# Reordering the stores and loads of one DMA queue in an RMSNorm kernel that repeats its rows

## The chip, the core and the metric

The kernel runs on one core of a Trainium2 chip. The metric is the device time of one execution in microseconds, over several timed runs. A profiled execution of each kernel gives the trace. Its span is some 1.7 to 1.8 us shorter than the timed figure, so spans are compared with spans and times with times.

## The reference

```python
def reference(x, gamma):                      # x: 8 x 512 x 2048, float32
    x_rep = np.repeat(x, 2, axis=1)           # each row twice
    rms = np.sqrt((x_rep ** 2).mean(axis=-1, keepdims=True) + 1e-6)
    return (x_rep / rms * gamma[None, None, :]).astype(np.float32)
```

The input is 33.6 MB, the output, with each row twice, 67.1 MB.

## The kernel before

Eight tiles of 512 rows. A tile occupies a buffer of 128 partitions x 8 rows; the load (4.19 MB) fills the upper four rows, the compute writes each row's result twice over the buffer, the store (8.39 MB) sends all eight rows out. There are three buffers, so load 3 must wait until store 0 has landed, load 4 for store 1, and so on. All large transfers are issued by SP, one after the other in program order: when SP waits for one issue, all issues behind it wait as well.

```python
rows = ctx.enter_context(tc.tile_pool(name="rows", bufs=3))
# ...
def load(i, eng, parts=1):
    y = rows.tile([P, K * R, D], f32, name="y")
    step = K // parts
    for k in range(0, K, step):
        at = K * (R - 1) + k
        eng.dma_start(out=y[:, at : at + step, :], in_=x_t[i, :, k : k + step, :])
    ys.append(y)

def store(i, k0, k1):
    nc.sync.dma_start(out=out_t[i, :, R * k0 * D : R * k1 * D], in_=ys[i][:, R * k0 : R * k1, :] ...)
# ...
def compute(i):
    for k in range(K):
        scale(i, k, square(i, k))             # squares on ACT, scaling on DVE
    repeat(i, 0, K // 2, nc.scalar.copy)      # half of the second copies on ACT
    repeat(i, K // 2, K, nc.vector.tensor_copy)
# ...
load(0, nc.sync, parts=2)
# ... gamma, eps ...
load(1, nc.sync)
load(2, nc.sync)
loads_after = {2: (3, 4, 5), 4: (6, 7)}
for i in range(ntiles):
    compute(i)
    store(i, 0, K)
    for j in loads_after.get(i, ()):
        load(j, nc.sync)
```

## Time and profile before

| What | Before |
|---|---|
| time, median of the first 3 runs | 239.39 us |
| span of the profiled run | 237.9 us |
| share of the span in which the SP queue's packets filled the 16 DMA engines | 98.5% |
| busy share of the vector and the scalar engine | 41%, 42% |

The prediction below shows the main lines. Two more views: the first is the busy tenths of the two compute engines in 40 slices of the span: 9 is busy, 0 is idle.

```profile
DVE  0049999960000000059999960000199990000000
ACT  2697999900000000099999920000599960000000
```

The compute comes in three blocks: tiles 0 to 2, tiles 3 to 5, tiles 6 and 7. Between them both engines stand still for some 30 to 50 us, waiting for a load. The second is the timeline of ACT at the start of the second block; in brackets is the idle time before it and what ended it.

```profile
101.18 1.88 ACT L64 ACTIVATE sq<-y 128x2048 f32<-128x2048 f32 x1 [53.03 <-DMA y<-in_x_dram]
```

ACT stood still for 53.03 us until load 3 landed.

### The profile page before, as it was taken

Reading aid. Unit: us, or ns where it says so; the run is one execution under the profiler, and the core shown is the slowest. Engines: PE = TensorE matmul, PEld = TensorE weight load, DVE = VectorE, ACT = ScalarE, POOL = GpSimd, SP = SyncE. Lnnn points to the kernel's source line nnn. Section 1 sums busy time; section 2 is a strip of 40 time slices with the busy share of each in tenths; the row PEclk is TensorE's granted clock in tenths of the full one; section 3 lists DMA queues with packets and bytes.
Section 4 is the critical chain, followed back from the end, with each engine's and each line's share of the span. In section 5 each row is a group of like instructions: output and inputs, shape, how many; then the busy total and the mean of one; then the engine's idle time right before and its main releaser. Section 6 shows DMA issues by size and latency. Waiting matters only on the chain.

```text
span 237.9 us, 287 instructions
## 1 busy us (share of the span) xinstructions
DVE 96.5 (41%) x73; ACT 101.0 (42%) x106; POOL 2.5 (1%) x5
## 2 busy tenths in 40 slices
DVE  0049999960000000059999960000199990000000
ACT  2697999900000000099999920000599960000000
POOL 0030000000000000000000000000000000000000
DMA  7999998989899998999998999989998989999994
GB/s 265 436 446 441 441 441 353 530 353 496 386 452 430 397 485 353 441 441 441 441 518 364 464 419 430 452 369 430 435 518 364 518 364 485 397 452 430 408 474 176
DMA packets 2464, 100.69 MB, mean 423 GB/s; under 512 B 279, under 2 KB 285, under 8 KB 286
## 3 DMA queue, kind: packets, MB, share of 16 engines
q1 hardware_dynamic: 2448, 100.66, 98.5%
q14 instruction: 2, 0.02, 0.0%
q10 hardware_dynamic: 14, 0.01, 0.0%
HBM read 33.56 MB, written 67.11 MB: 423 GB/s over the span
## 4 chain that ended last, share of the span: by engine, by line
DMA 58%; ACT 12%; DVE 9%; issue 1%; POOLq 1%; ACTq 1%; SPq 0%
DMA y<-in_x_dram 33%; DMA out_dram<-y 21%; ACT sq L64 8%; DVE y L74 7%; DMA gamma_b<-in_gamma_dram 4%; ACT y L81 3%; DVE y L81 2%; ACT rms L68 1%; POOLq L136 1%; ACTq L95 1%; DVE rstd L73 0%; POOLq L96 0%; SPq L56 0%
## 5 line engine op out<-in xcount | busy, mean ns | idle before, releaser
L64 ACT ACTIVATE sq<-y 128x2048 f32<-128x2048 f32 x32 | 59.7, 1865 | 87.8 <-DMA y<-in_x_dram 87.8
L74 DVE SCALAR_TENSOR_TENSOR y<-y,rstd,gamma_b 128x2048 f32<-128x2048 f32 x32 | 75.3, 2352 | 4.1 <-POOL gamma_b L96 3.0
L73 DVE RECIPROCAL rstd<-rms 128x1 f32<-128x1 f32 x32 | 5.0, 158 | 94.6 <-ACT rms L68 94.3
L81 ACT COPY y<-y 128x4096 f32<-128x4096 f32 x8 | 28.7, 3590 | 1.4 <-DVE y L74 1.4
L81 DVE COPY y<-y 128x4096 f32<-128x4096 f32 x8 | 18.3, 2294 | 0.3
L68 ACT ACTIVATE rms<-ss,eps_t 128x1 f32<-128x1 f32 x32 | 9.4, 295 | 1.0
L64 ACT ACTIVATION_READ_ACCUMULATOR sq<-y 128x1 f32 x32 | 6.0, 187 | 0.0
L64 ACT ACT_TABLE_LOAD x1 | 1.3, 1283 | 3.0 <-issue 3.0
L96 POOL PARTITION_BROADCAST gamma_b<-gamma_b x1 | 2.3, 2294 | 12.2 <-DMA y<-in_x_dram 12.2
L68 ACT ACT_TABLE_LOAD x1 | 1.3, 1283 | 0.0
L98 DVE MEMSET eps_t<- 128x1 f32 x1 | 0.1, 59 | 0.8 <-PEq L125 0.8
L125 POOL MEMSET const-uint8-127<- 128x1 uint8 x1 | 0.1, 102 | 0.0
L125 POOL MEMSET const-bfloat16-1.0<- 128x1 bf16 x1 | 0.1, 101 | 0.0
L125 POOL MEMSET const-float32-0.0<- 128x1 f32 x1 | 0.1, 98 | 0.2 <-issue 0.2
L125 POOL MEMSET const-float32-1.0<- 128x1 f32 x1 | 0.1, 98 | 0.0
## 6 DMA issues: line engine op xcount, KB each, us to landing
y<-in_x_dram SPq DMA_DIRECT2D x7, 4096.0 KB, 14.6
y<-in_x_dram SPq DMA_DIRECT2D x2, 2048.0 KB, 7.4
out_dram<-y SPq DMA_DIRECT2D x8, 24.4
gamma_b<-in_gamma_dram ACTq DMA_DIRECT2D x6, 1.0 KB
gamma_b<-in_gamma_dram ACTq DMA_DIRECT2D x1, 2.0 KB
```

The lines of the kernel that those rows point to most:

```text
L64: nc.scalar.activation(out=sq[:], in_=ys[i][:, K * (R - 1) + k, :], func=Act.Square, accum_out=ss[:])
L68: nc.scalar.activation(out=rms[:], in_=ss[:], func=Act.Sqrt, scale=inv_d, bias=eps_t[:])
L73: nc.vector.reciprocal(out=rstd[:], in_=rms[:])
L74: nc.vector.scalar_tensor_tensor(out=ys[i][:, R * k, :], in0=ys[i][:, K * (R - 1) + k, :], scalar=rstd[:], in1=gamma_b[:], op0=Alu.mult, o ...
L81: copy(out=y_r[:, k0:k1, 1, :], in_=y_r[:, k0:k1, 0, :])
L95: nc.scalar.dma_start(out=gamma_b[0:1, c0:c1], in_=gamma[c0:c1].partition_broadcast(1))
L96: nc.gpsimd.partition_broadcast(out_ap=gamma_b[:], in_ap=gamma_b[0:1, :])
L98: nc.vector.memset(eps_t, eps)
L125: nc = _bacc.Bacc("TRN2", target_bir_lowering=False, num_devices=1)
L136: with _tile.TileContext(nc) as tc:
```

## The change

```diff
-    loads_after = {2: (3, 4, 5), 4: (6, 7)}
+    loads_after = {1: (3, 4), 4: (5, 6, 7)}
```

SP's order becomes: three loads at the start, two stores, two loads, three stores, three loads, three stores. The intent is to let tiles 3 and 4 be loaded one store earlier, so that the compute engines wait less for them. No transfer is added, removed or resized.

## The prediction

> **What bounds the kernel now.** I first read the page of the profile of the kernel before: the busy shares, the slices and the DMA queues.
>
> ```profile
> span 237.9 us, 287 instructions
> DVE 96.5 (41%) x73; ACT 101.0 (42%) x106; POOL 2.5 (1%) x5
> ...
> DMA  7999998989899998999998999989998989999994
> ...
> q1 hardware_dynamic: 2448, 100.66, 98.5%
> ...
> HBM read 33.56 MB, written 67.11 MB: 423 GB/s over the span
> ```
>
> The two compute engines work for about 41% of the span each. The SP queue's packets keep the 16 DMA engines busy for 98.5% of it, and only the first and the last slice show a real dip. So the sum of bytes sets the time, and there are at most 1.5% of 237.9 us, some 3.6 us, of idle DMA time that any order could win back. Most of that is the start (nothing has been issued) and the end (the last stores land), which the change doesn't touch.
>
> Next I read the chain of work that ended last, in order of time, for the pace of a transfer. The columns are start, length and what.
>
> ```profile
> 27.05 25.77 DMA out_dram<-y
> ...
> 52.84 48.32 DMA y<-in_x_dram
> ...
> 115.86 24.36 DMA out_dram<-y
> 140.22 0.02 issue
> 140.24 29.08 DMA y<-in_x_dram
> 169.32 0.02 issue
> 169.34 2.01 ACT sq L64 x2
> ```
>
> The reader should see two landings, 48.32 us and 29.08 us apart, with issue gaps of 0.02 us. Between 52.84 (store 0 landed) and 101.16 (load 3 landed) the queue holds store 1, store 2 and load 3: two stores of 8.39 MB and one load of 4.19 MB, 20.97 MB, so 434 GB/s. Between 140.24 (store 3 landed) and 169.32 (load 6 landed) it holds store 4 and load 6: 12.58 MB in 29.08 us, 433 GB/s. Stores and loads therefore cost the same for a byte: a store about 19.36 us, a load about 9.68 us. Nothing else passes in between, however the two are mixed.
>
> Last I read the timeline of SP, which issues every large transfer, in short windows.
>
> ```profile
> 39.22 0.34 SPq L56 DMA_DIRECT2D out_dram<-y  x1
> 51.39 0.33 SPq L56 DMA_DIRECT2D out_dram<-y  x1
> 52.84 0.34 SPq L52 DMA_DIRECT2D y<-in_x_dram  x1
> 91.56 0.33 SPq L52 DMA_DIRECT2D y<-in_x_dram  x1
> 115.86 0.34 SPq L56 DMA_DIRECT2D out_dram<-y  x1
> 128.25 0.34 SPq L56 DMA_DIRECT2D out_dram<-y  x1
> ```
>
> These are the issues of store 1, store 2, load 3, load 5, store 3 and store 4 (load 4 is merged with another line). Loads go out the moment a store lands. An issue takes 0.34 us of SP. What matters is only that each issue comes before the engines have emptied what was issued earlier.
>
> **What the Trainium skill says.** "DMA: Bandwidth & Descriptors", section "Queues, rings and completion order": on each of the 16 engines the descriptors of one issuing queue are consumed in ring order. So the order in which SP issues is the order in which transfers get the engines, and SP's wait for one landing doesn't stop what is already queued. The trace agrees: load 3, issued at 52.84, landed only after stores 1 and 2. The same page, section "Where 436 GB/s comes from", gives 435 GB/s as the fabric's ceiling; the 433 to 434 GB/s above is at it, so I expect no hidden rate to gain. "HBM Reference", section "Specifications (TRN2)", says that a core streaming alone measures about 425 GB/s, bounded by its 16 DMA engines; the mean of 423 GB/s over this span agrees. Neither page gives a cost for turning from reading to writing, and the two rates above leave no room for a large one.
>
> **The change part by part.** It removes, adds and shortens no transfer: 9 load issues and 8 store issues stay. DVE, ACT and POOL run the same instructions in the same order (I compared the two programs; only SP's order differs). Load 5 moves from before store 3 to behind store 4, and store 2 goes from before load 3 to behind load 4. The work is to place each issue against the queue. I start from the landing of store 0, at 52.84 in both, since nothing up to there changes, and add 19.36 for a store and 9.68 for a load. Estimated landings of the new order: store 1 72.2, load 3 81.9, load 4 91.6, store 2 110.9, store 3 130.3, store 4 149.6, load 5 159.3, load 6 169.0, load 7 178.7, store 5 198.1, store 6 217.4, store 7 236.8. This needs every issue to come in time, so I check them one by one.
>
> Load 3 waits for store 0 (52.84), while store 1, issued at 39.22, keeps the engines busy until 72.2. Load 4 waits for store 1, to 72.2; at that moment only load 3 is queued, worth 9.68 us. Store 2's data has been ready since 51.4, so it follows load 4 after another 0.45 us of issuing, before 73. How long before an issue gives data? The page's issue table has a first 2 MB load that landed in 7.4 us, of which its own bytes take 4.8 at the pace above, so 2.6 us covers start and landing together. 9.68 less 2.6 leaves 7 us of margin.
>
> Store 3 needs tile 3's compute. In the trace before, load 3 landed at 101.16 and store 3 was issued at 115.86: 14.70 us. Now that gives 81.9 + 14.7 = 96.6, against engines busy to 110.9. Store 4 followed store 3's issue by 12.39 us (128.25 less 115.86), which gives 109.0, against 130.3. Load 5 waits for store 2 (110.9), load 6 for store 3 (130.3), load 7 for store 4 (149.6). The first two sit behind store 4; at the third, loads 5 and 6 are still queued, 19.4 us of work.
>
> Store 5 is the tight one: 159.3 + 14.7 = 174.0, while loads 6 and 7 keep the engines busy to 178.7. That is 4.7 us ahead, 2.1 us after the 2.6 us for start and landing. But this is the same pattern as store 3 in the kernel before (issued 115.86, loads 4 and 5 busy until about 120.5), and that one left no bubble. The change only moves the block of three loads, whose two later loads hide the first tile's compute, from the first refill to the second. Store 6 comes near 186.4 against 198.1, store 7 near 199 against 217.4. **The sum:** 0 us saved, 0 us added. The last landing, 236.8 by this count, is within 1.1 us of the span of before, whose own count by the same steps is equal, because both are 52.84 plus seven stores and five loads: 52.84 + 7 x 19.36 + 5 x 9.68 = 236.8.
>
> **The rivals.** First, a **bubble at load 4 or at store 5**. For it: the queue is shallower there; before, stores 1 and 2 lay behind store 0. Had the latency of an issue been 5 us instead of 2.6, store 5 would leave about 0.3 us, and were tile 5's compute 3 us longer, 1 us. Against it: the issues are on time by the count, and the same pattern ran clean in the old order. It would make 240 to 242.
>
> Second, a **change in the cost of switching between reads and writes**. Both orders have two switches from store to load and three from load to store, so a cost per switch cancels. What could differ is what runs beside it: compute traffic falls into other transfers. If that slowed or freed a few packets, I would expect 0.5 us either way, 238.9 to 239.9.
>
> Third, a **gain from earlier compute**: tiles 3 and 4 start about 20 us earlier, and store 3 gets more lead. For it: SP's wait for the data of stores is long. Against it: the engines are fully busy through that wait, so an earlier finish has nowhere to go. Even all idle DMA time away gives only 1.5%, and the start and end can't go, so it can't reach 2% faster. It would make 238.5 at best.
>
> **The range and the chances.** I predict the same time, 239.4 us. The three timed runs lie within 0.2 us, so the 8 in 10 range is set by the second rival and a small bubble: 238.8 to 240.3. Faster by over 2% (below 234.6) would need less than the bytes cost: 0.005. Slower by over 2% (above 244.2) would need a bubble of 4.8 us that I find nowhere: 0.015. The rest, 0.98, is within 2%.
>
> **What would show it right or wrong.** In the changed profile: the DMA queue's share stays within 0.5 points of 98.5%; the DMA row shows no digit under 8 except the first and last slices; load 3 lands near 82, not 101; ACT's long idle time before tile 3's squares shrinks by about 19 us and a longer one appears before tile 5; store 5 is issued near 174, load 7 near 150, and the three loads of that block still take about 29 us. A DMA slice of 7 or less near 82 or near 179 would show the first rival and prove me wrong on the margins. A full DMA row with a span off by more than 1 us would mean that the pace of packets depends on the order, which I hold to be false.

## The result and the profile after

The changed kernel took 239.75 us (median of 6 runs, 239.57 to 239.90), the kernel before 239.41 us (6 runs, 239.30 to 239.70). The ratio is 1.0012, with a 95% interval of 0.9999 to 1.0025: the same time. Ratios here are the mean time of one kernel's runs over that of the other's of the same rounds, so they are not quite the ratio of the medians.

The page of the changed kernel answers line by line to that of before:

```profile
span 238.1 us, 287 instructions
...
DVE  0059999950000089993000000008999993000000
ACT  2697999900000299990000000029999990000000
...
DMA  7999998989899999989898999999998989899994
...
q1 hardware_dynamic: 2448, 100.66, 98.5%
```

The compute has moved: its second block is two tiles long and earlier, its third is three tiles long and begins earlier. The DMA row is as full as before and its share is the same to the tenth of a per cent. The timeline of ACT shows the move in numbers:

```profile
82.03 1.88 ACT L64 ACTIVATE sq<-y 128x2048 f32<-128x2048 f32 x1 [34.00 <-DMA y<-in_x_dram]
159.37 1.88 ACT L64 ACTIVATE sq<-y 128x2048 f32<-128x2048 f32 x1 [52.48 <-DMA y<-in_x_dram]
```

Tile 3 starts 19.15 us earlier (82.03 against 101.18), about the time of one store, after a wait of 34.00 us instead of 53.03. The long wait, 52.48 us, now comes before tile 5. ACT's whole idle time before its squares went from 87.8 to 90.2 us: the waiting was moved, not removed.

The timeline of SP, in short windows, gives the issues of load 3, store 2, store 3, load 7, store 5 and store 6:

```profile
53.02 0.34 SPq L52 DMA_DIRECT2D y<-in_x_dram  x1
72.97 0.34 SPq L56 DMA_DIRECT2D out_dram<-y  x1
96.72 0.34 SPq L56 DMA_DIRECT2D out_dram<-y  x1
149.66 0.33 SPq L52 DMA_DIRECT2D y<-in_x_dram  x1
174.06 0.34 SPq L56 DMA_DIRECT2D out_dram<-y  x1
186.44 0.34 SPq L56 DMA_DIRECT2D out_dram<-y  x1
```

The chain of waits gives the pace:

```profile
72.97 38.07 DMA out_dram<-y
111.06 48.29 DMA y<-in_x_dram
159.35 0.02 issue
```

From 111.06 (store 2 landed) to 159.35 (load 5 landed) the queue held stores 3 and 4 and load 5, the same 20.97 MB as the 48.32 us of before, and took 48.29 us.

### The profile page after: what moved, and what is told of

It reads as the page before. It is cut to its first block, busy times and chain, and to the rows that moved or that the text cites. A ratio compares the mean times of both kernels' runs of the same rounds, so it can differ in the third digit from the quotient of the medians.

```text
span 238.1 us, 287 instructions
## 1 busy us (share of the span) xinstructions
DVE 96.5 (41%) x73; ACT 101.0 (42%) x106; POOL 2.5 (1%) x5
## 4 chain that ended last, share of the span: by engine, by line
DMA 54%; DVE 14%; ACT 11%; issue 2%; POOLq 1%; ACTq 1%; SPq 0%
DMA out_dram<-y 30%; DMA y<-in_x_dram 20%; DVE y L74 11%; ACT sq L64 7%; DMA gamma_b<-in_gamma_dram 4%; ACT y L81 3%; DVE y L81 2%; POOLq L136 1%; ACT rms L68 1%; ACTq L95 1%; DVE rstd L73 0%; SPq L52 0%; SPq L56 0%; POOLq L96 0%
## 5 line engine op out<-in xcount | busy, mean ns | idle before, releaser
L64 ACT ACTIVATE sq<-y 128x2048 f32<-128x2048 f32 x32 | 59.7, 1865 | 90.2 <-DMA y<-in_x_dram 90.2
L81 DVE COPY y<-y 128x4096 f32<-128x4096 f32 x8 | 18.4, 2294 | 0.3
```

The costliest lines, as they stand in the source:

```text
L64: nc.scalar.activation(out=sq[:], in_=ys[i][:, K * (R - 1) + k, :], func=Act.Square, accum_out=ss[:])
L81: copy(out=y_r[:, k0:k1, 1, :], in_=y_r[:, k0:k1, 0, :])
```

## The experiments

In all runs the trace's records of single DMA packets were read too: a transfer is cut into packets, and of each transfer every one of the 16 engines moves eight. A packet of a store (65,536 bytes) has a median of 2,418 ns on its engine, one of a load (32,768 bytes) 1,213 ns, in both kernels and in all experiments. Below, a hole or a gap is a time in which the engines stand idle, given as the mean over the 16 engines.

### The changed kernel again, and a control

The changed kernel was submitted unaltered, and so was the kernel before, as if it were a changed one.

> The changed kernel once more, unaltered, with more rounds, to see whether the 0.34 us between the medians (239.75 against 239.41) is real. Theory A (the order of the queue costs nothing as long as something is always queued): 239.4 to 239.8, ratio 0.999 to 1.002, and no more than noise between the two. Rival B (another order costs a few slow packets at its switches): ratio 1.001 to 1.002 again, with an interval that leaves out 1.

> A control: the kernel before, submitted as if it were a changed one. The changed kernel came out 1.0012 and 1.0014 times as long. If this is only how the comparison is made, the control shows about 1.001 as well. If the new order costs a few tenths of a us, the control shows 1.000, within 0.0008.

The changed kernel took 239.69 us, ratio 1.0014 (1.0001 to 1.0027); the control took 239.61 us, ratio 1.0004 (0.9989 to 1.0018). Twice the changed kernel came out 0.3 us longer, but the control's own interval covers both ratios. A difference of 0.1% may exist; these runs don't settle it. Nothing below rests on it.

### A queue that runs dry at each load

```diff
-    loads_after = {1: (3, 4), 4: (5, 6, 7)}
+    loads_after = {0: (3,), 1: (4,), 2: (5,), 3: (6,), 4: (7,)}
```

Each load now waits for the store issued just ahead of it, with nothing queued in between.

> One store, then one load that waits for this very store to land, five times. The SP queue stands at each of these loads with nothing else queued, so the DMA engines fall idle from the end of the store to the first data of the load. Theory A: five gaps of about 2.0 to 2.6 us each (store's landing, issue, start of data), so +10 to +13 us: 249.5 to 252.5, and gaps to be seen near 53, 84, 115, 147 and 178 us. Rival B (what costs is a switch between reading and writing, not an empty queue): this order has five switches from store to load and six from load to store, eleven against five, so it would add six times the cost of a switch, and the next run, which has the same switches with a full queue, would be just as slow.

It took 257.80 us, ratio 1.0769: 18.4 us longer than before, and above the expected 249.5 to 252.5. The DMA row of its page:

```profile
DMA  7999999969989499996999769999699997998986
```

The low digits in the middle are the gaps. The timeline of SP has the issues of load 3, store 1 and load 4:

```profile
52.78 0.33 SPq L52 DMA_DIRECT2D y<-in_x_dram  x1
53.27 0.34 SPq L56 DMA_DIRECT2D out_dram<-y  x1
85.44 0.33 SPq L52 DMA_DIRECT2D y<-in_x_dram  x1
```

From 52.78 to 85.44 are 32.66 us for a load and a store, which take 9.68 + 19.36 = 29.04 us in an unbroken queue: 3.6 us lost each time. The packet records split this. The engines were idle for 1.8 to 2.1 us at each of the five gaps, a little less than the expected 2.0 to 2.6. The rest I had not expected: the packets of the five loads took 1.75 us longer per gap (the packets of all loads sum to 77.84 us per engine, against 69.09 in the changed kernel, over five gaps). They are slow at two places, the first packet after the gap (mean 1,871 ns for load 3) and the last one before the next store (2,137 ns). So an empty queue costs about 3.7 us here, twice its idle time.

### The same alternation with a queue that is never empty

```diff
-    loads_after = {1: (3, 4), 4: (5, 6, 7)}
+    loads_after = {1: (3,), 2: (4,), 3: (5,), 4: (6,), 5: (7,)}
```

> The same alternation of one load and one store as in the run whose queue runs dry, but started one store later, so that a store or a load is always queued behind the one awaited: store 0, store 1, load 3, store 2, load 4, and so on. Theory A: every issue is on time by the count (the tightest is store 6, ready about 2.1 us ahead after the latency), so 239.4 to 239.9 in spite of eleven switches instead of five. Rival B: six more switches at c each; with c 0.5 us it would be 242.4, with c 1 us 245.4. Rival C (more mixing is better, reads and writes overlapping at a switch): below 239.0.

It took 240.37 us (6 runs, 239.74 to 241.43), ratio 1.0045 (1.0025 to 1.0065). With the same eleven switches between reading and writing as the run above, 17.4 of the 18.4 us are gone. So the cost was the empty queue and not the switches. But 1.0 us remains, above theory A's upper figure of 239.9. The DMA row shows where:

```profile
DMA  7999998989899989899998999899989898999992
```

It is full up to the last slice, which falls from 4 to 2: the engines end unevenly. (This profiled execution took 241.08 us, more than the median of its six, so it shows the effect large.) For each landing, the packet records tell by how much the slowest of the 16 engines was behind the mean of all (us, worked out from the records, at the end of the last load before a store):

```
                            load 2   first refill    later loads          last store
before                       0.32        0.36           0.90                0.89
changed kernel               0.23        0.48           1.02                1.01
alternation, queue full      0.27        0.45    0.57, 0.82, 1.28, 2.09     2.08
```

The mean end of the last store's packets hardly moved (235.9, 235.9 and 236.1 us). What grew is the slowest engine's lag. It grows mostly at the ends of loads, where a few packets are slow, and is not made up in these three runs, since each engine has the same eight packets to move in every transfer. In this profile more ends of loads before a store came with more such slips; that they make the 1.0 us of the timed runs as well is likely, but only one execution was profiled.

### Only one load behind the load that is computed

```diff
-    loads_after = {1: (3, 4), 4: (5, 6, 7)}
+    loads_after = {2: (3, 4), 4: (5, 6, 7)}
```

> Only one line of the schedule is changed: loads 3 and 4 after store 2, and load 5 with 6 and 7 after store 4. Only one load (9.68 us) then lies behind load 3 while tile 3 is computed (14.70 us). Theory A with the count of margins: store 3 is late by 14.7 + 1.7 to 2.6 of start - 9.7 = 6.7 to 7.6 us, so 246.1 to 247.1, one gap near 111 us and none elsewhere. Rival (the change was neutral because the compute doesn't matter at all, the queue always finds work): 239.4.

It took 248.93 us, ratio 1.0396 (1.0383 to 1.0410): 9.2 us longer than the changed kernel, where 6.7 to 7.6 had been expected. The DMA row has one hole, the 3 near 111 us:

```profile
DMA  7999989899997979973797999899999898989994
```

The timeline of SP shows store 3 (and store 4, merged with it) coming late:

```profile
115.69 12.73 SPq L56 DMA_DIRECT2D out_dram<-y  x2
```

The hole itself is 6.6 us of idle engines, 0.1 us short of the count. The rest of the spans' difference (246.9 less 238.1, 8.8 us) is again in slow packets: 0.93 us per engine in the loads and 0.78 us in the stores, at the first change to a load and the first change to a store after the hole, and 0.5 us in the lag of the slowest engine at the end.

### The same order with short compute

```diff
     def compute(i):
+        if i >= 3:
+            nc.scalar.copy(out=ys[i][:, 0 : K // 2, :], in_=ys[i][:, K : K + K // 2, :])
+            nc.vector.tensor_copy(out=ys[i][:, K // 2 : K, :], in_=ys[i][:, K + K // 2 :, :])
+            return
...
-    loads_after = {1: (3, 4), 4: (5, 6, 7)}
+    loads_after = {2: (3, 4), 4: (5, 6, 7)}
```

The result is wrong: tiles 3 to 7 are copied, not normalised.

> The order with loads 3 and 4 after store 2, that took 248.9, with the same short compute of tiles 3 to 7 (wrong result on purpose). Theory A: its gap was compute (14.7 us) sticking out from behind one load (9.7 us); with 3.7 us it is covered, so the whole loss of 9.5 us goes, slow packets after the gap too: 239.4 to 240.0. Rival (that order is slow in itself, by its queue or its slow packets): some part of the loss stays, 241 to 249.

It took 239.55 us, ratio 1.0003 (0.9989 to 1.0017). The whole loss is gone, slow packets included. That order lost time only because the compute of tile 3 stuck out from behind load 4.

### The changed order with short compute

The same edit of `compute` with the changed kernel's order, also wrong.

> The changed kernel, wrong result on purpose: tiles 3 to 7 are not normalised, one copy on each of the two engines replaces the 14.7 us of compute by some 3.7 us. Theory A (the transfers alone set the time): 239.4 to 239.8, nothing gained although five tiles are ready 11 us earlier. Rival (earlier compute lets stores go sooner): faster by a us or more. Slips of single DMA engines could shift it by 0.3 us, if compute traffic causes them.

It took 239.66 us, ratio 1.0009 (0.9996 to 1.0022), against 239.69 of the changed kernel with its full compute. ACT's busy time fell from 101.0 to 57.6 us and DVE's from 96.5 to 47.6 us, for nothing. In the profiled runs the lag of the slowest engine at the end was smaller, 0.49 us here and 0.53 us in the run above, against 0.77 to 1.08 us in the five profiled runs of the two kernels and of the run with one more copy. That hints that compute beside the transfers makes some of the slips. The timed figures don't show it. The spans of the timed executions do lie lower, 237.2 to 237.6 us in both runs with short compute against 237.8 to 238.2 in the repeat of the changed kernel, but the timed figures stand 2.2 us above these spans instead of 1.7 to 1.8, for a reason that no run here shows. So it stays a hint.

### Tile 5 made later, by one and by three copies

```diff
         compute(i)
+        if i == 5:
+            for _ in range(1):          # 3 in the second run
+                repeat(i, K // 2, K, nc.vector.tensor_copy)
         store(i, 0, K)
```

> The changed kernel, with the last copy of tile 5 on the vector engine done once more (2.29 us), so that store 5 is issued near 176.3 instead of 174.06, while load 7 keeps the engines busy to about 178.6. [...]Theory A with margins: 2.3 us ahead is still enough: 239.7, no gap. Rival (the end of the compute of tile 5 is on the path that sets the time): +2.3, 242.0.

> As the run with one more copy of tile 5, with three (6.9 us), so store 5 is issued near 180.9, 2.3 us after load 7 has ended. Theory A with margins: a gap of 2.3 + 1.5 to 1.9 = 3.8 to 4.2 us near 179 to 183 us, so 243.4 to 244.0. Only stores follow this gap, so the slow load packets that followed each gap in the runs whose queue ran dry should not add to it; if they do, it is 245 or more. Rival (end of tile 5 on the path all along): +6.9, 246.6.

With one more copy it took 239.61 us, ratio 1.0010 (0.9997 to 1.0023): 2.2 us more of compute on the tightest tile cost nothing. With three it took 243.07 us, ratio 1.0149 (1.0135 to 1.0164), 3.4 us more than the changed kernel. The timeline of SP has the issue of store 5, here with one more copy:

```profile
176.28 0.34 SPq L56 DMA_DIRECT2D out_dram<-y  x1
```

Here with three:

```profile
180.97 0.34 SPq L56 DMA_DIRECT2D out_dram<-y  x1
```

The DMA rows of the two pages, first with one more copy:

```profile
DMA  7999998989899999989898999999998989899894
```

Then with three:

```profile
DMA  7999999999999999898989898999949898989894
```

A store 5 issued at 176.28 leaves no hole; one issued at 180.97 leaves one, the 4 near 180 us. By the packet records it is 4.0 us, inside the expected 3.8 to 4.2, and no slow load packets followed; only stores came after it. But the 1.5 to 1.9 us in that sum are not the time from an issue to its first data, as they were meant to be: that was 0.9 us here (store 5, mean of the 16 engines). The other 0.8 us is that the engines had ended load 7 at 177.9 us on average, before the 178.7 at which the count had it landing. That the time rose by 3.4 us only, below the expected 3.7 at least, has a plain reason: the hole made the engines start together again, so the slowest one ended 0.1 us behind the mean and not 1.0.

### Half of the last store

```diff
-        store(i, 0, K)
+        store(i, 0, K if i < 7 else K // 2)
```

Half of the last tile's output is missing.

> The changed kernel, with only the first half of tile 7 stored (4.19 MB of output missing, wrong on purpose). Theory A (time is bytes at one pace): 9.67 us less, 229.8 to 230.2. Rival (part of the end is a wait for compute, or a fixed tail): less gained, 231 or more.

It took 230.15 us, ratio 0.9616 (0.9602 to 0.9630): 9.54 us less than the changed kernel's 239.69, for 4.19 MB, which take 9.66 us at 434 GB/s. Taking bytes away shortens the kernel at the pace of the transfers; in the runs above, taking compute away didn't.

No experiment points to a version that beats both kernels. Packets alone make 234.4 us per engine (the sum of the records in both), of a span of 238 us. What is left lies at its two ends: the engines begin 2.0 us after its start on average; the last packet ends 1.2 us before its end, and the mean engine 0.9 to 1.0 us before that. (These sum to a little over the span, as the records of packets that follow one another overlap by some ns.)

## Why the prediction was right

The prediction was 239.4 us with a range of 238.8 to 240.3; the measured median was 239.75 us, 0.35 us above the centre.

- **The bound.** It held that bytes at one pace set the time. The half store (9.54 us less for half of a store) and the short compute (no gain with some 43 us less of ACT's work) show this directly.
- **The count of landings and issues.** Predicted and measured issues: store 3 at 96.6 and 96.72, store 4 at 109.0 and 109.09, load 7 at 149.6 and 149.66, store 5 at 174.0 and 174.06, store 6 at 186.4 and 186.44, store 7 near 199 and 198.83. The method (landing of before, plus 19.36 or 9.68 us a transfer, plus 14.70 us of compute) was good to 0.3 us for the issues, load 4 the worst (72.2 and 72.47).
- **The margins.** Store 5 was called the tight one, 4.7 us ahead of the end of load 7 and 2.1 us after start and landing. The delay of 2.2 us was absorbed and that of 6.9 us made a hole of 4.0 us, so the true margin is 2.9 us (6.9 less 4.0). The term that was off is the 2.6 us for start and landing: it counted the wait from the last packet to the landing and the slow first packets of the kernel too. What had to be taken off the 4.6 us between the issue (174.06) and the counted landing (178.7) was 1.7 us: 0.9 us from the issue to the first data, and 0.8 us by which the engines end, on average, before the counted landing. The error was on the safe side.
- **The first rival, a bubble,** didn't come about in the changed kernel, but the run with one load behind tile 3 shows that it was no straw man: the same two loads one store later cost 9.2 us. Its price in the text left out the slow packets that follow a hole when loads come after it (1.75 us per gap, 1.7 us after the one hole). At store 5, where only stores follow, a hole of 4.0 us cost 3.4 us, and nothing came on top.
- **The second rival, switches.** That the cost of switches cancels between the two orders held within the 0.3 us that the control doesn't separate from noise. But the text's "Nothing else passes in between, however the two are mixed" was too strong: six more switches cost 1.0 us, in the one profile of that run by slips of single engines at the ends of loads.
- **The third rival, gain from earlier compute,** is refuted by the changed kernel itself, with tile 3 done 19 us earlier, and by the short compute.

Not settled: why the packets are slow at the first load and at the first change from load to store after the engines have stood idle, and hardly at later ones (the change to store 0 cost 0.9 and 1.0 us per engine in the two kernels, later changes below 0.1); what makes single engines slip; and whether the 0.3 us is real.

## What to carry to other kernels

When one queue keeps the DMA engines full, the idle time of the compute engines is not a reserve: ask of each issue whether it comes before the queue runs empty, with a lead in hand (here about 1.7 us before the counted landing of what is queued, of which 0.9 us is the time from the issue to the first data). Work out the margin of each wait before reordering; a neutral order and one that costs 9 us can differ by one load. Once each margin was positive, a further reordering had nothing to give here, and one with more switches took 1.0 us; only fewer bytes made the kernel faster.

## What the Trainium skill lacked or had wrong

- "DMA: Bandwidth & Descriptors", section "Latency and other measured facts", gives about 600 ns as the first byte's latency for transfers issued from SP or ACT. It doesn't say from which moment. The packet records agree with it if it counts from the end of the issue: after the holes, the first packets of stores 3 and 5 began 0.84 us after the start of the issue, 0.50 us after its end, and those of the loads in the run with five gaps 0.95 to 0.98 us after the start, 0.62 to 0.65 us after the end. No page gives, for transfers issued from SP, the lead that a schedule needs: here about 1.7 us before the counted landing of what is queued.
- No page has the further cost of a queue that ran dry: on top of the idle time, packets of the next load were slow at its start and at its end, 1.75 us per gap in the run with five gaps.
- No page has a figure for how far the 16 engines of one queue drift apart over a kernel: the slowest was 0.9 us behind the mean at the end of the kernel before and 2.1 us with eleven switches.
